# Output projection of a hybrid encoder block: element-wise work of the Strassen-like pairs on VectorE alone, the first pair's second tile loaded inside the attention

## The chip, the cores and the metric

The kernel runs on one core of one Trainium2 chip. The metric is the device time of one execution in microseconds (us). The core's engines are TensorE (PE; its weight loads appear as PEld), VectorE (DVE), ScalarE (ACT), GpSimd (POOL) and SyncE (SP), each with an instruction queue of its own, and 16 DMA engines that they issue to.

## The reference

One layer of an encoder on x of shape (1, 2048, 1024), all in float32:

```
xn = rmsnorm(x);  z = xn @ w_in                      # q, k, v, pool input, forget logits
fox  = forgetting_attention(q, k, v, f)              # 8 heads of 64 channels, causal
pool = multiscale_pool(p_in)                         # 512 channels
h = x + concat(fox, pool) @ w_out                    # the output projection, w_out (1024, 1024)
h = h + memory_cross_attention(rmsnorm(h), mem)      # 4 heads, 256 memory tokens
h = h + swiglu(rmsnorm(h))                           # 1024 -> 2816 -> 1024
```

The change lies in the fourth line, `h = x + concat(fox, pool) @ w_out`, and in the end of the attention ahead of it.

## The kernel before

**Precision.** Every float32 operand of a matmul is split into a rounded part (hi) and a remainder (lo): ACT casts the raw values into hi, then another engine forms lo = raw - hi (`split`, L199 and L55). A product is three matmuls for each of four blocks of 128 (`mm3`, L60 to L62: hi x hi, lo weights x hi, hi x lo).

**Output projection in pairs.** The 16 token tiles of 128 rows are taken in eight pairs of tiles (i, i + 4). With the tiles' fox halves (x11, x21) and pool halves (x12, x22) and the halves of w_out, a pair's 2x2 block product is formed with seven products in place of eight (a Strassen-Winograd scheme). It needs four sums of operands, formed anew for each pair in `pair_ops`:

- s1 = x21 + x22, s2 = s1 - x11, s3 = x11 - x21, s4 = x12 - s2;
- the weights' sums t1 to t4 were formed earlier in the kernel and stored to DRAM; `out_weights` loads t3, t4 and the block b22, and splits them; b11, b21, t1 and t2 are loaded and split in the attention's last units.

A pair's products, in PE's order, are: x11 by b11, x22 of the earlier pair by t4, x12 by b21, s4 of the earlier pair by b22, s2 by t2, s1 by t1, s3 by t3. Each is 12 matmuls of 128x512. Three PSUM banks a pair hold them: bank a takes x11, then s2, then s3, then (in the next pair) x22 on top of one another; bank b s1, then s4; bank c x12. So between these products a bank has to be read out. `begun` (L1326) adds a bank to the rows of x that were loaded into a tile o; `ended` (L1331) adds a further bank to it, and then POOL stores o (L1332) to `h1d` in DRAM. The output blocks are called o11, o12, o21 and o22 here (first or second tile, first or second half of the columns). o12 is begun after s2, o22 after s1, and both read banks that the next products go into.

**Where the operands lie.** `pair_raw` loads the four parts of a pair into one tile of 4 x 512 (`praw`, two buffers): x11, x12, x21, x22 in places 0 to 3 (`raw`). The sums are written over parts that are done with: s1 over x22, s3 over x21, s2 over place 0, s4 over place 1. s1 and s2 are formed on DVE, s3 and s4 on POOL (L1292, `tt(..., pool)`). hi and lo go into places ww0 to ww10 (`out_place`), in turn.

**The first pair.** Its first tile is loaded in the attention's last unit already (`load_first_pair`, into the upper half of a value tile v), and split nine steps later (`split_first_pair`); its operands x11 and x12 stay there. Its second tile is loaded by `pair_raw(0)` into `praw`, which gets the buffer of the last head's values and so has to wait for the attention's last matmul. The remainders of t4 and b22 are formed on POOL, those of t3 on DVE.

**What sets the order.** In the attention the order on DVE, ACT and SP is that of the program text; `later(n, fn)` puts a function n steps of that text's loop later. In the output projection only SP's order is that of the text (`in_order(EN.SP)`), PE's is so everywhere, and DVE, ACT and POOL are ordered by the scheduler that builds the program. Each engine then works through its queue strictly in order. On SP a load that waits for its buffer holds up all that follow. `x_rows` takes its tiles from six buffers, for o12 from two (`oh`), so its loads wait for stores of earlier pairs; the next pair's four loads stand behind them.

Of the kernel before, what the change touches and what calls it, by code (L numbers as in the profile page):

```python
# [8 lines left out]
F32 = mybir.dt.float32  # L9
F32R = mybir.dt.float32r  # L10
AF = mybir.ActivationFunctionType
ALU = mybir.AluOpType
# [4 lines left out]
P = 128  # L17
# [23 lines left out]
def block_kernel(ctx: ExitStack, tc: tile.TileContext, x, xT, memT, cols, rows, w_qkvf, w_p, w_pool, w_out,  # L41
# [4 lines left out]
    act, dve, pool, pe, sp = nc.scalar, nc.vector, nc.gpsimd, nc.tensor, nc.sync  # L46

    def opened(stack, name, bufs=1, **kw):
        return stack.enter_context(tc.tile_pool(name=name, bufs=bufs, reuse_waits="tile", **kw))

    def f(ap):
        return ap.bitcast(F32)

    def sub_hi(lo, src, hi, eng=None):
        (eng or dve).tensor_tensor(out=lo, in0=src, in1=f(hi), op=ALU.subtract)  # L55
# [51 lines left out]
    catT = [dr.tile([FOXW, 512], F32, name=f"catT{n}") for n in range(4)]  # L107
    poolT = [dr.tile([POOLW, 512], F32, name=f"poolT{n}") for n in range(4)]
# [84 lines left out]
    def split_gain(hi, lo, raw, gain):  # L193
        act.activation(hi, raw, AF.Copy, scale=gain)
        dve.scalar_tensor_tensor(out=lo, in0=raw, scalar=gain, in1=f(hi), op0=ALU.mult, op1=ALU.subtract)

    def split(hi, lo, raw, gain=None, eng=None):
        if gain is None:
            act.copy(hi, raw)  # L199
            sub_hi(lo, raw, hi, eng)  # L200
        else:
            split_gain(hi, lo, raw, gain)

    tt = lambda o, a_, b_, op, e_=dve: e_.tensor_tensor(out=o, in0=a_, in1=b_, op=op)
# [31 lines left out]
    with xstack, in_order(EN.DVE, EN.Activation, EN.Pool, EN.SP):  # L236
# [540 lines left out]
        hp = opened(hps, "hp")  # L777
# [12 lines left out]
    ob, first_pair = {}, {}  # L790
    pair_tiles = lambda p_: (8 * (p_ // 4) + p_ % 4, 8 * (p_ // 4) + p_ % 4 + 4)

    def load_part(raw, src, i):

        sp.dma_start(raw, src[i // 4][:, i % 4 * P:(i % 4 + 1) * P].rearrange("(k p) t -> p k t", p=P))

    def load_first_pair():
        v = hp.tile([P, NT, P], F32R, tag="v", name="v", bufs=2)
        raw = [f(v[:, 4 * n:4 * n + 4]) for n in range(2)]
        lo = hp.tile([P, 4, P], F32R, tag="cm", name="x12l", bufs=3)  # L800
        hi = hp.tile([P, 4, P], F32R, tag="cm", name="x12h", bufs=3)
        load_part(raw[0], catT, 0)
        load_part(raw[1], poolT, 0)
        first_pair["x11"] = v[:, 8:12], v[:, 12:16]
        first_pair["x12"] = hi[:], lo[:]
        return raw

    def split_first_pair(raw):
        first_pair["raw"] = [r.rearrange("p k t -> p (k t)") for r in raw]
        for r, nm in zip(raw, ("x11", "x12")):  # L810
            hi, lo = first_pair[nm]
            act.copy(hi, r)
            sub_hi(lo, r, hi)
            first_pair[nm] = tuple(t_.rearrange("p k t -> p (k t)") for t_ in (hi, lo))

    with ExitStack() as c0:
        tpool = opened(c0, "tpool")
# [8 lines left out]
        def later(n, fn):  # L826
            due.append([n, fn])
# [139 lines left out]
        def halves(pl):  # L967

            t_ = [slab(n, pl, F32R) for n in range(4)]
            return [(t_[n // 4][:, n % 4 * 512:(n % 4 + 1) * 512], t_[2 + n // 4][:, n % 4 * 512:(n % 4 + 1) * 512])  # L970
                        for n in range(8)]

        def load_out_quarters():

            parts = halves(hpa)
            for n, (hi, lo) in enumerate(parts):
                ob[("b11", "b21")[n // 4], n % 4] = hi, lo

                def load(n=n, hi=hi, lo=lo):
                    raw = spool.tile([P, 512], F32, tag="s0", name="wor", bufs=4)  # L980
                    sp.dma_start(raw[:], w_out[n * P:(n + 1) * P, :512])
                    later(14, lambda: split(hi, lo, raw[:], eng=pool))

                later(4 + 4 * n, load)

        def load_out_sums():
            parts = halves(hpb)
            for c in range(4):
                nm = ("t2", "t1")[c // 2]
                raw = spool.tile([P, 1024], F32, tag="s1", name="wos", bufs=4)  # L990
                sp.dma_start(raw[:].rearrange("p (k c) -> p k c", k=2), osum[nm][:, 2 * (c % 2):2 * (c % 2) + 2])
                for n in range(2 * c, 2 * c + 2):
                    ob[nm, n % 4] = hi, lo = parts[n]
                    later(11 + 3 * n, lambda hi=hi, lo=lo, v=raw[:, n % 2 * 512:(n % 2 + 1) * 512]: split(hi, lo, v))

        def all_scores():
            for un in units:
                h, b = un["u"]
                if b == (1 if h else 2) and h + 1 < H:
                    heads[h + 1] = load_head(h + 1, (hpa, hpb)[(h + 1) % 2])  # L1000
                if b == 3 and h + 1 < H:

                    heads[h + 1] += (load_values(h + 1),)
                elif h + 1 == H and b == 3:

                    load_out_quarters()
                un["head"] = heads[h]
                yield from score_items(un)
            raw = load_first_pair()
            later(9, lambda: split_first_pair(raw))  # L1010
            load_out_sums()

        def all_values():
# [232 lines left out]
    with ExitStack() as c0:  # L1246
# [16 lines left out]
        def out_weights(nm):  # L1263

            if nm == "t3":
                t_ = wdp.tile([P, 4, 512], F32, tag="wd", name="wor", bufs=1)
                raw = [t_[:, 2 * n:2 * n + 2] for n in range(2)]
            else:
                raw = [f(pair_place(n + (5 if nm == "t4" else 7))[:]) for n in range(2)]
            for n, r in enumerate(raw):  # L1270
                sp.dma_start(r, w_out[FOXW + n * B:FOXW + (n + 1) * B, 512:].rearrange("(k p) c -> p k c", p=P)
                             if nm == "b22" else osum[nm][:, 2 * n:2 * n + 2])
                for k in range(2):
                    t_ = obp.tile([P, 2, 512], F32R, name=f"o{nm}{2 * n + k}")
                    ob[nm, 2 * n + k] = t_[:, 0], t_[:, 1]
                    split(t_[:, 0], t_[:, 1], r[:, k], eng=dve if nm == "t3" else pool)

        def pair_raw(p_):
            v = hp.tile([P, 4, 512], F32, tag="v", name="praw", bufs=2)
            x11, x12, x21, x22 = raw = [v[:, n] for n in range(4)]  # L1280
            if p_ == 0:
                x11, x12 = first_pair.pop("raw")
            for n in range(0 if p_ else 2, 4):
                r = raw[n]
                load_part(r.rearrange("p (k t) -> p k t", k=4), (catT, poolT)[n % 2], pair_tiles(p_)[n // 2])
            return (x11, x12, x21, x22), raw

        def pair_ops(p_, parts, raw):

            x11, x12, x21, x22 = parts  # L1290
            x = {}
            tt = lambda o, a_, b_, op, e_=dve: e_.tensor_tensor(out=o, in0=a_, in1=b_, op=op)  # L1292

            def put(nm, src):
                x[nm] = out_place()
                split(*x[nm], src)

            if p_:
                put("x11", x11)
                put("x12", x12)  # L1300
            else:
                x.update(first_pair)
            put("x22", x22)
            tt(x22, x21, x22, ALU.add)
            tt(x21, x11, x21, ALU.subtract, pool)
            tt(raw[0], x22, x11, ALU.subtract)
            put("s2", raw[0])
            put("s1", x22)
            put("s3", x21)
            tt(raw[1], x12, raw[0], ALU.subtract, pool)  # L1310
            put("s4", raw[1])
            return x

        def product_o(ps, xop, wop, first):
# [89 lines left out]
    with mstack, ExitStack() as c0:  # L1404
# [67 lines left out]
        with in_order(EN.SP):  # L1472
# [5 lines left out]
            for n in range(2, NT + 1):  # L1478
# [349 lines left out]
```

## Time and profile before

| what | value |
|---|---|
| runs | 2582.59, 2586.41, 2586.48 us; median 2586.41 us |
| the profiled execution | 2578.56 us, its span 2576.9 us |
| busy of the span | PE 97%, PEld 84%, DVE 67%, ACT 50%, POOL 32% |
| mean granted clock of TensorE | 0.995 |
| the stretch in question | output projection, from 845.87 us (first product) to about 1036 us |

A line of the timeline gives the start and the duration in us, the engine, the line of the kernel, the operation, what is written and read (out<-in), the shape, how many are merged in the row, and in brackets the idle time before it and what ended that. A wait that is put down to DVE or ACT means that PE stood still until that instruction had finished. Names without numbers are tiles: `obk` the PSUM banks of the projection, `ww` the places of hi and lo, `praw` the raw parts, `ot` and `ob` the split t3 or t4 and b22, `o` the output rows. In PE's rows `qs` and `kh` are the weights b11, t2 and b21, t1 in the buffers of the attention's heads.

### The profile page before, as it was taken

To read this page: it belongs to the slowest core of one execution; us is meant where nothing else is said; L and a number is where in the kernel's file an instruction comes from. 1 tells how busy PE (TensorE), PEld (TensorE's weight loads), DVE (VectorE), ACT (ScalarE), POOL (GpSimd) and SP (SyncE) were. 2 spreads that over 40 slices of the span, in tenths; PEclk is the share of its full clock that TensorE was granted. 3 is DMA by queue.
4 is the path that set the end of the run, shared out by engine and by line. 5 is a ranking of instruction groups with operands and counts; after the bars stand their busy time and mean duration, and the time that the engine had idled before them with its cause. 6 is when DMAs were issued, how large, how long until landed. Compare 5 with 4: busy or idle time off the path is not lost.

```text
span 2576.9 us, 37301 instructions
## 1 busy us (share of the span) xinstructions
PE 2510.7 (97%) x12909; PEld 2154.4 (84%) x12909; DVE 1734.8 (67%) x2998; ACT 1299.4 (50%) x2487; POOL 822.0 (32%) x1135
## 2 busy tenths in 40 slices
PE   8999998999999899999999999999999999999998
PEld 8999997788887687888778888888888888888887
DVE  4466745899998754555877778756766666665554
ACT  5555446788889422655543433334543333333443
POOL 0022424455555522444424545430001222212000
PEclk9999999999999999999999999999999999999999
DMA  8755767645433546222465555447773323325665
GB/s 276 215 178 156 216 192 210 187 123 156 130 109 92 185 150 214 74 87 95 174 224 181 174 178 190 151 164 271 244 266 109 122 104 108 122 98 185 228 214 186
DMA packets 246766, 434.01 MB, mean 168 GB/s; under 512 B 30000, under 2 KB 119856, under 8 KB 238896
## 3 DMA queue, kind: packets, MB, share of 16 engines
q1 hardware_dynamic: 213104, 322.54, 39.5%
q0 software_dynamic: 33472, 109.08, 11.7%
q8 instruction: 102, 1.67, 0.3%
q14 instruction: 88, 0.72, 0.1%
HBM read 294.02 MB, written 137.50 MB: 167 GB/s over the span
## 4 chain that ended last, share of the span: by engine, by line
PE 49%; issue 8%; DVE 2%; ACT 1%; DMA 1%; POOL 1%; SPq 0%; POOLq 0%; DVEq 0%; ACTq 0%
PE bk L62 13%; PE bk L60 13%; PE bk L61 13%; PE mmps L60 2%; PE mmps L62 2%; PE mmps L61 2%; PE tp L1039 1%; DVE ww L55 0%; PE obk L60 0%; PE obk L61 0%; PE obk L62 0%; DMA xraw<-hTd 0%; POOL out_dram L1721 0%; DMA wqr<-in_w_mem_q_dram 0%; DMA h<-h1d 0%
## 5 line engine op out<-in xcount | busy, mean ns | idle before, releaser
L55 DVE TENSOR_TENSOR ww<-draw,ww 128x512 fp32r<-128x512 f32 x308 | 205.2, 702 | 155.6 <-ACT ww L199 155.1
L199 ACT CAST ww<-draw 128x512 fp32r<-128x512 f32 x308 | 179.5, 620 | 218.8 <-PE bk L62 174.5
L55 DVE TENSOR_TENSOR ww<-graw,ww 128x512 fp32r<-128x512 f32 x220 | 177.8, 815 | 105.9 <-ACT ww L199 105.5
L61 PE MATMUL bk<-ww,ww 128*128 128x512 f32 x616 | 239.6, 389 | 0.0
L60 PE MATMUL bk<-ww,ww 128*128 128x512 f32 x616 | 239.6, 389 | 0.0
L62 PE MATMUL bk<-ww,ww 128*128 128x512 f32 x616 | 239.6, 389 | 0.0
L199 ACT CAST ww<-graw 128x512 fp32r<-128x512 f32 x220 | 135.9, 622 | 181.8 <-PE bk L62 159.8
L55 DVE TENSOR_TENSOR pl<-tp,ph 128x512 fp32r<-128x512 f32 (+3 forms) x296 | 176.7, 599 | 27.8 <-ACT ph L952 26.0
L871 ACT ACTIVATE s<-s,mx 128x1024 f32<-128x1024 f32 (+2 forms) x192 | 173.6, 905 | 7.7 <-DVE mx L865 7.1
L936 PE MATMUL tp<-ident,s 128*128 128x128 f32 x1088 | 171.5, 273 | 3.4 <-DVE pl L55 3.0
L60 PE MATMUL zps<-wh,xhi 128*128 128x386 f32 x512 | 174.6, 341 | 0.0
L62 PE MATMUL zps<-wh,xl 128*128 128x386 f32 x512 | 173.7, 339 | 0.0
L61 PE MATMUL zps<-wl,xhi 128*128 128x386 f32 x512 | 173.2, 338 | 0.0
L952 ACT CAST ph<-tp 128x512 fp32r<-128x512 f32 (+3 forms) x296 | 148.7, 514 | 38.3 <-PE tp L936 32.8
L936 PEld LDWEIGHTS tp<-ident,s 128*128 128x128 f32 x1088 | 133.9, 141 | 31.6 <-DVE pl L55 6.6
L1721 POOL DMA_DIRECT2D out_dram<-o x32 | 17.3, 542 | 382.5 <-DVE o L1718 381.6
L62 PE MATMUL bk<-qs,ww 128*128 128x512 f32 x352 | 137.2, 390 | 1.1 <-DVE ww L55 1.1
L60 PE MATMUL bk<-qs,ww 128*128 128x512 f32 x352 | 137.9, 392 | 0.3 <-ACT s L1640 0.3
L61 PE MATMUL bk<-kh,ww 128*128 128x512 f32 x352 | 137.0, 389 | 0.0
L60 PE MATMUL bk<-kl,ww 128*128 128x512 f32 x352 | 136.9, 389 | 0.0
L61 PE MATMUL bk<-cb,ww 128*128 128x512 f32 x352 | 136.9, 389 | 0.0
L62 PE MATMUL bk<-kl,ww 128*128 128x512 f32 x352 | 136.9, 389 | 0.0
(613 smaller groups left out, 7261.9 us busy)
## 6 DMA issues: line engine op xcount, KB each, us to landing
graw<-in_w_gu_dram SPq DMA_DIRECT2D x44, 1024.0 KB, 5.4
draw<-in_w_down_dram SPq DMA_DIRECT2D x66, 256.0 KB, 4.3
xl<-in_xT_dram SPq DMA_DIRECT2D x64, 256.0 KB, 4.5
wdr<-in_w_down_dram SPq DMA_DIRECT2D x22, 512.0 KB, 4.6
jl<-in_x_dram SPq DMA_DIRECT2D x32, 256.0 KB, 7.0
vd<-cb SPq DMA_DIRECT2D x16, 512.0 KB, 3.5
cb<-cd SPq DMA_DIRECT2D x8, 1024.0 KB, 7.8
v<-vd SPq DMA_DIRECT2D x8, 1024.0 KB, 5.4
```

What stands on the lines that cost most here:

```text
L55: (eng or dve).tensor_tensor(out=lo, in0=src, in1=f(hi), op=ALU.subtract)
L60: pe.matmul(ps, lhsT=sh, rhs=mh, start=first, stop=False, skip_group_check=goes_on)
L61: pe.matmul(ps, lhsT=sh, rhs=ml, start=False, stop=False, skip_group_check=goes_on)
L62: pe.matmul(ps, lhsT=sl, rhs=mh, start=False, stop=last, skip_group_check=goes_on)
L199: act.copy(hi, raw)
L871: act.activation(s[:, sl], s[:, sl], AF.Exp, bias=ng, scale=-1.0, accum_out=l[:, q, g:g + 1])
L936: pe.transpose(tp[:, q * P:(q + 1) * P], unit["rows"][q][:, j * P:(j + 1) * P], ident[:])
L952: act.copy(ph[:, sl], tp[:, sl])
L1039: pe.transpose(tp[:, e_], src[:, q + e_], ident[:])
L1721: pool.dma_start(out[rows_, cs], o)
```

## The change

All element-wise work of the projection goes to DVE: the sums s3 and s4 of every pair (`tt` loses its engine argument) and the remainders of t4 and b22 (`split` without `eng`). The sums get places of their own: in the pairs from the second on s1 goes into a tile of the small pool `cm` (three buffers, used by the attention's masks before), s2 into place 0, s3 into place 2, s4 over x12. Their order in the text changes: the three sums s1, s3, s2 first, then the splits of s2, s1, s3 and x22.

For the first pair the parts of the second tile are loaded sixteen steps after the request of the first (`load_first_second`), inside the attention: x21 into a `cm` tile, x22 over the raw x12, which has been split by then. As s4 still needs the raw x12, `pair_raw(0)` loads that part again into `praw`, and the other three places take s1, s2 and s3.

```diff
     def split_first_pair(raw):
-        first_pair["raw"] = [r.rearrange("p k t -> p (k t)") for r in raw]
         for r, nm in zip(raw, ("x11", "x12")):
...
+    def load_first_second(raw):
+        x21 = hp.tile([P, 4, P], F32, tag="cm", name="x21", bufs=3)[:]
+        load_part(x21, catT, pair_tiles(0)[1])
+        load_part(raw[1], poolT, pair_tiles(0)[1])
+        first_pair["raw"] = [r.rearrange("p k t -> p (k t)") for r in (raw[0], x21, raw[1])]
...
             later(9, lambda: split_first_pair(raw))
+            later(16, lambda: load_first_second(raw))
...
-                    split(t_[:, 0], t_[:, 1], r[:, k], eng=dve if nm == "t3" else pool)
+                    split(t_[:, 0], t_[:, 1], r[:, k])
...
             if p_ == 0:
-                x11, x12 = first_pair.pop("raw")
-            for n in range(0 if p_ else 2, 4):
-                r = raw[n]
+                load_part(raw[1].rearrange("p (k t) -> p k t", k=4), poolT, pair_tiles(0)[0])
+                x11, x21, x22 = first_pair.pop("raw")
+                return (x11, raw[1], x21, x22), raw[2], (raw[0], raw[3])
+            for n, r in enumerate(raw):
                 load_part(r.rearrange("p (k t) -> p k t", k=4), (catT, poolT)[n % 2], pair_tiles(p_)[n // 2])
-            return (x11, x12, x21, x22), raw
+            return raw, hp.tile([P, 512], F32, tag="cm", name="s1r", bufs=3)[:], (raw[0], raw[2])
...
-            put("x22", x22)
-            tt(x22, x21, x22, ALU.add)
-            tt(x21, x11, x21, ALU.subtract, pool)
-            tt(raw[0], x22, x11, ALU.subtract)
-            put("s2", raw[0])
-            put("s1", x22)
-            put("s3", x21)
-            tt(raw[1], x12, raw[0], ALU.subtract, pool)
-            put("s4", raw[1])
+            tt(s1, x21, x22, ALU.add)
+            tt(s3, x11, x21, ALU.subtract)
+            tt(s2, s1, x11, ALU.subtract)
+            put("s2", s2)
+            put("s1", s1)
+            put("s3", s3)
+            put("x22", x22)
+            tt(x12, x12, s2, ALU.subtract)
+            put("s4", x12)
```

The order in which the engines' queues then stand is shown with the steps of the prediction. Lines after the new function have higher numbers: the sums move from L1292 to L1300, `begun` from L1326 to L1334, `ended` from L1331 to L1339.

More of the change, by code (lines that the diff above doesn't have):

```diff
@@ L1275, in out_weights, with pair_ops @@
                     ob[nm, 2 * n + k] = t_[:, 0], t_[:, 1]
-                    split(t_[:, 0], t_[:, 1], r[:, k], eng=dve if nm == "t3" else pool)
+                    split(t_[:, 0], t_[:, 1], r[:, k])
         def pair_raw(p_):
             v = hp.tile([P, 4, 512], F32, tag="v", name="praw", bufs=2)
-            x11, x12, x21, x22 = raw = [v[:, n] for n in range(4)]
+            raw = [v[:, n] for n in range(4)]
             if p_ == 0:
-                x11, x12 = first_pair.pop("raw")
-            for n in range(0 if p_ else 2, 4):
-                r = raw[n]
+                load_part(raw[1].rearrange("p (k t) -> p k t", k=4), poolT, pair_tiles(0)[0])
+                x11, x21, x22 = first_pair.pop("raw")
+                return (x11, raw[1], x21, x22), raw[2], (raw[0], raw[3])
+            for n, r in enumerate(raw):
                 load_part(r.rearrange("p (k t) -> p k t", k=4), (catT, poolT)[n % 2], pair_tiles(p_)[n // 2])
-            return (x11, x12, x21, x22), raw
-        def pair_ops(p_, parts, raw):
+            return raw, hp.tile([P, 512], F32, tag="cm", name="s1r", bufs=3)[:], (raw[0], raw[2])
+        def pair_ops(p_, parts, s1, free):
             x11, x12, x21, x22 = parts
+            s2, s3 = free
             x = {}
-            tt = lambda o, a_, b_, op, e_=dve: e_.tensor_tensor(out=o, in0=a_, in1=b_, op=op)
+            tt = lambda o, a_, b_, op: dve.tensor_tensor(out=o, in0=a_, in1=b_, op=op)
             def put(nm, src):
```

## The prediction, made before the changed kernel was run

> **What bounds the kernel now.** I read the page first, then the windows around the output projection, then PE's timeline there, and last DVE's.
>
> ```profile
> span 2576.9 us, 37301 instructions
> PE 2510.7 (97%) x12909; PEld 2154.4 (84%) x12909; DVE 1734.8 (67%) x2998; ACT 1299.4 (50%) x2487; POOL 822.0 (32%) x1135
> 850.00:860.00 10.00, 4.90 (x15) 3.35 (x14) 8.63 (x12) 5.14 (x9) 4.59 (x5) 0.83 0.83 273
> 860.00:870.00 10.00, 9.24 (x33) 6.91 (x32) 4.37 (x7) 5.70 (x10) 8.69 (x7) 0.83 1.04 310
> 960.00:970.00 10.00, 7.35 (x32) 5.73 (x31) 8.09 (x12) 2.39 (x4) 4.18 (x5) 0.96 0.21 79
> 970.00:980.00 10.00, 10.00 (x40) 8.14 (x39) 2.48 (x4) 1.31 (x3) 0.54 (x1) 0.87 0.79 233
> ```
>
> PE is busy for 97% of the span, so only time in which PE waits or runs slowly can be won. The windows' columns are length, then busy time of PE, PEld, DVE, ACT and POOL, the granted clock, the DMA share and GB/s. Around 850 PE loses half of a window, and the clock falls to 0.83; around 965 it happens again, less. Both places lie in the output projection. These are its starts of products, and what PE waited for:
>
> ```profile
> 845.87 0.39 PE L60 MATMUL obk<-qs,v 128*128 128x512 f32 x1
> 855.14 0.50 PE L60 MATMUL obk<-qs,ww 128*128 128x512 f32 x1 [3.65 <-ACT ww L199]
> 857.32 0.79 PE L62 MATMUL obk<-qs,ww 128*128 128x512 f32 x1 [1.44 <-DVE ww L55]
> 868.06 0.50 PE L60 MATMUL obk<-qs,ww 128*128 128x512 f32 x1
> 869.55 0.50 PE L62 MATMUL obk<-qs,ww 128*128 128x512 f32 x1 [0.76 <-DVE ww L55]
> 888.75 0.50 PE L60 MATMUL obk<-ot,ww 128*128 128x512 f32 x1 [3.04 <-DVE o L1326]
> 910.64 0.39 PE L60 MATMUL obk<-qs,ww 128*128 128x512 f32 x1
> 929.68 0.39 PE L60 MATMUL obk<-qs,ww 128*128 128x512 f32 x1
> 947.04 0.50 PE L60 MATMUL obk<-ot,ww 128*128 128x512 f32 x1 [0.88 <-DVE o L1326]
> 969.05 0.69 PE L60 MATMUL obk<-ot,ww 128*128 128x512 f32 x1 [2.65 <-DVE o L1326]
> 973.50 0.40 PE L60 MATMUL obk<-qs,ww 128*128 128x512 f32 x1
> 1011.91 0.50 PE L60 MATMUL obk<-ot,ww 128*128 128x512 f32 x1 [1.98 <-DVE o L1326]
> ```
>
> From 910.64 to 929.68 lies pair 3 with its seven products: 19.04 us without a wait, so 2.72 us a product. From the first product (845.87) to that of s3 in pair 7 (1011.91) stand 53 products, 144.2 us, and 0.8 us of transposes; it took 166.0, so 21.0 us are lost. By place: 8.6 up to 868.06, where pair 1 begins five products after the start, and about 1.1 in the product there (0.76 and two start-ups); 3.2 in pair 1 (3.04 and a start-up of 0.2); 1.1 and 2.9 in pairs 4 and 5; 1.7 after that, since the product at 969.05 took 4.45 us and not 2.72 (the 0.87 of the windows); 2.2 in pair 7.
>
> **Why PE waits.** From pair 1 on every wait is for the evacuation L1326 of the output block o12 (first tile, second half of the columns), ahead of the product of s3, which goes into the same bank. DVE works strictly in its order, and o12 stands behind the next pair's splits. Pair 5, with pair 6's splits:
>
> ```profile
> 955.70 0.69 DVE L55 TENSOR_TENSOR ww<-praw,ww 128x512 fp32r<-128x512 f32 x1 [4.89 <-ACT ww L199]
> 959.84 0.69 DVE L55 TENSOR_TENSOR ww<-praw,ww 128x512 fp32r<-128x512 f32 x1 [0.99 <-ACT ww L199]
> 960.56 0.69 DVE L1292 TENSOR_TENSOR praw<-praw 128x512 f32<-128x512 f32 x1
> 962.72 0.69 DVE L1292 TENSOR_TENSOR praw<-praw 128x512 f32<-128x512 f32 x1 [1.46 <-POOL praw L1292]
> 963.93 2.07 DVE L55 TENSOR_TENSOR ww<-praw,ww 128x512 fp32r<-128x512 f32 x2
> 967.12 0.68 DVE L1331 TENSOR_TENSOR o<-obk,o 128x512 f32<-128x512 f32 x1
> 967.72 0.68 DVE L55 TENSOR_TENSOR ww<-praw,ww 128x512 fp32r<-128x512 f32 x1
> 968.32 1.28 DVE L1326 TENSOR_TENSOR o<-obk,o 128x512 f32<-128x512 f32 x2
> 924.33 0.68 DVE L1331 TENSOR_TENSOR o<-obk,o 128x512 f32<-128x512 f32 x1
> 945.11 0.68 DVE L1331 TENSOR_TENSOR o<-obk,o 128x512 f32<-128x512 f32 x1
> L55 DVE TENSOR_TENSOR ww<-praw,ww x54: 675/688/1785, 850.5 to 1005.4; 128x512 fp32r<-128x512 f32 x54
> L1292 POOL TENSOR_TENSOR praw<-praw x14: 1282/1294/1624, 873.9 to 984.3; 128x512 f32<-128x512 f32 x14
> ```
>
> x22's split comes at 959.84, s1 at 960.56; then DVE waits 1.46 us for POOL's s3 before it may form s2, and the two splits at 963.93 take 2.07 us (1.29 without hindrance), one of them stretched while POOL forms s4. The last two rows (min, median and max in ns) say the same: a DVE split is 688 ns, up to 1785 beside a POOL sum of 1294. So o12 comes 8.5 us after x22's split. The other two L1331 rows are the last evacuation of the earlier pair's block (924.33, 945.11, 967.12): 20.8 and 22.0 us apart, while PE needs 19.04 a pair. Its store frees the buffer behind whose load the next operands queue on SP. DVE therefore falls back by some 1.8 us a pair until PE waits.
>
> **The change, part by part.**
>
> *Sums on DVE, kept apart.* In pairs 1 to 7 POOL loses two sums (1.29 us each), DVE gets two (0.69, started 0.60 apart: 967.12, 967.72, 968.32). DVE then has seven splits, four sums and seven evacuations, 18 x 0.60 = 10.9 of 19.04 us: not the bound. The order on DVE in pair 5 before (from x11's evacuation of pair 5, o_12383, to o12, o_12385; praw_12514 is pair 6's data):
>
> ```order
> L1326 TENSOR_TENSOR o_12383<-obk_12414,o_12383 128x512
> L55 TENSOR_TENSOR ww9_12531<-praw_12514,ww9_12531 128x512
> L1292 TENSOR_TENSOR praw_12514<-praw_12514 128x512 x2
> L1326 TENSOR_TENSOR o_12442<-obk_12278,o_12442 128x512
> L55 TENSOR_TENSOR ww6_12411<-praw_12378,ww6_12411 128x512
> L55 TENSOR_TENSOR ww0_12540<-praw_12514,ww0_12540 128x512
> L1331 TENSOR_TENSOR o_12383<-obk_12416,o_12383 128x512
> L55 TENSOR_TENSOR ww1_12543<-praw_12514,ww1_12543 128x512
> L1331 TENSOR_TENSOR o_12249<-obk_12279,o_12249 128x512
> L55 TENSOR_TENSOR ww10_12537<-praw_12514,ww10_12537 128x512
> L1326 TENSOR_TENSOR o_12385<-obk_12414,o_12385 128x512
> ```
>
> and after, the same stretch (o_12390 to o_12392; s1 into s1r_12526 stands in the row ahead of it):
>
> ```order
> L1334 TENSOR_TENSOR o_12390<-obk_12421,o_12390 128x512
> L1300 TENSOR_TENSOR praw_12521<-praw_12521 128x512
> L1300 TENSOR_TENSOR praw_12521<-s1r_12526,praw_12521 128x512
> L55 TENSOR_TENSOR ww0_12548<-praw_12521,ww0_12548 128x512
> L1334 TENSOR_TENSOR o_12449<-obk_12284,o_12449 128x512
> L55 TENSOR_TENSOR ww9_12542<-praw_12521,ww9_12542 128x512
> L1300 TENSOR_TENSOR praw_12521<-praw_12521 128x512
> L1339 TENSOR_TENSOR o_12390<-obk_12423,o_12390 128x512
> L55 TENSOR_TENSOR ww1_12551<-praw_12521,ww1_12551 128x512
> L1339 TENSOR_TENSOR o_12255<-obk_12285,o_12255 128x512
> L55 TENSOR_TENSOR ww10_12545<-s1r_12526,ww10_12545 128x512
> L1334 TENSOR_TENSOR o_12392<-obk_12421,o_12392 128x512
> ```
>
> The sums moved in, x22's split moved from ahead of s1 to behind s4, and nothing in the chain waits for POOL. From s1's start to o12 there are now 12 steps, 12 x 0.605 = 7.3 us, and to the earlier block's last evacuation 10 steps, 6.1 us. s1 can start when x22 has landed, about 0.7 before its split, at 959.1: o12 at 966.4 instead of 968.3, the evacuation at 965.2 instead of 967.1. That one takes back the 1.8 us a pair by which DVE falls behind, so the delay no longer builds up. I take the waits of pairs 4 and 5 and the slow product as gone: -5.7 us (1.1 + 2.9 + 1.7); if the 1.9 us are won once and the delay stays, pair 4's 1.1 go and 1.9 of pair 5's: -3.0.
>
> *Weights' splits.* Eight remainders of t4 and b22 move from POOL to DVE, 8 x 0.60 = 4.8 us, ahead of pair 1's first splits. They wait for loads:
>
> ```profile
> 833.66 0.32 SPq L886 DMA_DIRECT2D ld<-li  x1
> 835.96 0.45 SPq L892 DMA_DIRECT2D lbs<-ld  x1
> 846.07 0.37 SPq L795 DMA_DIRECT2D praw<-catT  x1
> 846.49 0.50 SPq L795 DMA_DIRECT2D praw<-poolT  x1
> 847.30 1.88 DVE L55 TENSOR_TENSOR cb<-wos,kh 128x512 fp32r<-128x512 f32 x3
> 847.46 3.13 POOL L904 TENSOR_TENSOR fo<-fo,lbs 64x512 f32<-64x512 f32 x1 [3.53 <-DVE fo L898]
> 849.88 0.62 ACT L199 CAST ww<-praw 128x512 fp32r<-128x512 f32 x1 [1.66 <-DMA praw<-poolT]
> 850.88 0.57 POOL L906 DMA_DIRECT2D catT<-fo  x1 [0.29 <-POOL fo L904]
> SPq L1271 <- DMA catT<-fo: 5.9, 1, 5.9
> 868.21 0.62 ACT L199 CAST ww<-praw 128x512 fp32r<-128x512 f32 x1 [0.20 <-DMA praw<-poolT]
> ```
>
> SP holds the second half of t4 for 5.9 us behind the attention's last store (850.88), with b22 and pair 1's operands queued after it; the queue is full (DMA share 1.04), and x12 of pair 1 lands only at 868.2. The eight splits lie beside these loads, so I cost them at nothing, and pair 1 cannot start before about 868 either way; with faster loads up to 4.8 us of them would show.
>
> *Pair 1.* In the new order 23 steps stand between x11's split (868.2 and 0.6 of ACT) and o12: 13.9 us, 882.7, done at 883.4; PE would come to s3 at 888.75 - 3.2 = 885.5. The wait goes, -3.2. Pair 2's operands must land meanwhile; if they are 1.5 us late, -1.7.
>
> *Pair 0.* The loads of x21 and x22 go on SP between the last store of the inverse row sums (833.66) and their load back (835.96), where SP waits for 2.0 us; two issues of 0.37 and 0.50 fit in. Behind them stands only that load, which POOL needs at 847.46. At 846.07 one load (x12 again) is left of two. s1 can run as soon as the value tile is free, at 846, ahead of the attention's last evacuation, which it holds up by 0.1 at most. But DVE's order is new:
>
> ```order
> L55 TENSOR_TENSOR cb_11134<-wos_11139,kh_11132 128x512
> L55 TENSOR_TENSOR cb_11134<-wos_11141,kh_11132 128x512 x2
> L1300 TENSOR_TENSOR praw_11692<-v_11126,x21_11339 128x512
> L1300 TENSOR_TENSOR praw_11692<-praw_11692,v_11126 128x512
> L1300 TENSOR_TENSOR praw_11692<-praw_11692 128x512
> L55 TENSOR_TENSOR ww0_11718<-praw_11692,ww0_11718 128x512
> L55 TENSOR_TENSOR ww1_11721<-praw_11692,ww1_11721 128x512
> L55 TENSOR_TENSOR ww2_11724<-praw_11692,ww2_11724 128x512
> L55 TENSOR_TENSOR ww3_11727<-v_11126,ww3_11727 128x512
> L55 TENSOR_TENSOR ww4_11731<-praw_11692,ww4_11731 128x512
> L1334 TENSOR_TENSOR o_11694<-obk_11766,o_11694 128x512
> ```
>
> where before this stood:
>
> ```order
> L55 TENSOR_TENSOR cb_11134<-wos_11141,kh_11132 128x512 x2
> L55 TENSOR_TENSOR ww0_11713<-praw_11689,ww0_11713 128x512
> L1326 TENSOR_TENSOR o_11692<-obk_11764,o_11692 128x512
> L1292 TENSOR_TENSOR praw_11689<-praw_11689 128x512
> L1331 TENSOR_TENSOR o_11692<-obk_11766,o_11692 128x512
> ```
>
> The evacuation of the first product moved behind three sums and five splits, and the product of s2 goes into the same bank. From 849.2 (last weight split): 3 x 0.6 and 0.1, then 5 x 0.6 and the evacuation of 0.7: 854.9. PE comes to s2 at 855 and not at 856.6 (857.32 less two matmuls), unless POOL's scaling (847.46) takes its 1.4 us in the middle: 856.3. Both are hidden again, since pair 1 starts with its loads at 868: 0, with ends of -1.0 (256 KB less at the 273 GB/s of the window) and +1.4 (the store at 850.88 that much later).
>
> *Pair 7.* Its wait hangs on the mem-query weights, whose loads start when pair 5's last block is stored. Those come about a microsecond earlier: -0.4, ends -2.2 and 0.
>
> Sum: 0 - 3.2 - 5.7 - 0.4 = -9.3 us; ends -12.1 and -3.3. The profiled execution took 2578.56 us (span 2576.9): 2569.3 for one like it. The runs' median is 2586.41, 7.9 above it, for no reason that this trace shows; I set the sum against the median: 2577.1. About 0.2%, 5.2 us, can be told from no change here.
>
> **The rivals.**
>
> *The clock.* After 2.65 us of waiting the product at 969.05 ran slowly, after 3.04 the one at 888.75 did not (first matmul 0.50, not 0.69). The Trainium skill ("TensorE: Matmul & The Clock Gate", Part 1) has a free-running window of 3.4 us, and half the clock after an idle one. By it a wait's place in the window decides beside its length; the two rows bear that out, though a wholly idle window was not needed here. In pair 0 PE now works through s2, s1 and s3 without a break (8.2 us) and then stands idle in one piece until 868, from 863.1 or 864.5, where before the long wait lay ahead of s2 and the slow matmuls after it (0.79 at 857.32) were hidden by the loads. If that makes pair 1's first products slow, 1.7 us are lost, at most twice: -7.6 or -5.9, some 2579.5.
>
> *A new wait in place of the old.* x11's evacuation, which lets s2 begin, now stands behind s1, and s1 needs the second tile's loads landed. If they still land as late as in pair 5 (959.1, 9.3 us after that pair's first product at 949.8, 947.04 and a product), PE waits for it or for o12 by a microsecond in pairs 4 to 6: half the gain of these goes, -9.3 + 3 to 5, some 2582. For it speaks the full queue, against it the shorter cycle.
>
> *Slower.* If the loads land later than 8.3 us into a pair, o12 (7.3 + 0.7 after) misses the 16.3 us (six products) at which s3 is due. At 11.4 us in each of pairs 2 to 6 that is 5 x 3.1 = 15.5 lost against 9.3 won: 2592.6. It would need an evacuation two microseconds later than now, and the chain got shorter.
>
> *It does nothing.* If pair 1's and pair 5's waits were the loads' and not the chain's, 2586.
>
> **How the numbers follow.** Forecast (-12 to -7.5) 0.48; the clock 0.2; a new wait 0.2; nothing 0.07; slower 0.05. Faster by more than 5.2 us are the first, three quarters of the clock and a third of the new wait: 0.70; slower 0.05; the rest, 0.25, is the same. The range reaches from 2571 (all waits gone, and 3 us of scatter as between the runs) to 2584.
>
> **What would show it.** After: no POOL sums in the projection; PE's waits on o12 in pairs 1, 4 and 5 under 0.5 us together, the clock 1.00 from 880 to 1000; the last evacuations 19.0 us apart; s2 of pair 0 waiting for L1334, not ACT; pair 1 still beginning near 868. Wrong would be waits of over 1 us a pair on L1334, or a second stretch at half clock after 868.

## The result, and the profile after

| what | before | after |
|---|---|---|
| median of six runs, us | 2583.09 | 2572.61 |
| lowest to highest, us | 2580.55 to 2586.48 | 2571.55 to 2575.98 |
| profiled execution, its span, us | 2576.9 | 2570.0 |

The ratio of the runs is 0.9957, with an interval of 0.9947 to 0.9967: the changed kernel is about 11 us faster. Forecast were 9.3 us less. The forecast time of 2577.1 us was counted from 2586.41, the median of three runs of the kernel before; that of all six is 2583.09. So of the 4.5 us that the forecast time is too high, 3.3 come from that median.

The head of the page of the changed kernel, and four windows of it (length, busy time of PE, PEld, DVE, ACT and POOL, granted clock, DMA share, GB/s):

```profile
span 2570.0 us, 37278 instructions
PE 2510.6 (98%) x12909; PEld 2156.2 (84%) x12909; DVE 1736.8 (68%) x3022; ACT 1298.8 (51%) x2487; POOL 789.2 (31%) x1111
850.00:860.00 10.00, 5.42 (x20) 4.18 (x19) 9.56 (x14) 4.15 (x8) 4.67 (x3) 0.86 0.76 260
860.00:870.00 10.00, 9.64 (x34) 7.38 (x33) 7.05 (x12) 6.53 (x12) 0.00 (x0) 0.80 1.03 310
960.00:970.00 10.00, 10.00 (x46) 8.29 (x45) 3.34 (x6) 1.25 (x2) 1.08 (x2) 1.00 0.75 227
970.00:980.00 10.00, 10.00 (x46) 8.29 (x45) 8.31 (x13) 2.40 (x4) 1.62 (x3) 1.00 0.35 122
```

PE's own time is the same (2510.6 against 2510.7). The hole around 965 with its slow clock is gone, that around 855 is not. PE's starts of products, as they were shown of before:

```profile
847.63 0.40 PE L60 MATMUL obk<-qs,v 128*128 128x512 f32 x1
857.86 0.77 PE L60 MATMUL obk<-qs,ww 128*128 128x512 f32 x1 [4.58 <-DVE o L1334]
869.03 0.39 PE L60 MATMUL obk<-qs,ww 128*128 128x512 f32 x1
871.77 0.50 PE L62 MATMUL obk<-qs,ww 128*128 128x512 f32 x1 [2.13 <-DVE ww L55]
890.54 0.39 PE L60 MATMUL obk<-qs,ww 128*128 128x512 f32 x1
985.74 0.39 PE L60 MATMUL obk<-qs,ww 128*128 128x512 f32 x1
1002.96 0.39 PE L60 MATMUL obk<-ot,ww 128*128 128x512 f32 x1
```

These two are the waits of over 0.3 us that are left; in pair 0 the slow clock is left too. From 890.54 to 985.74 pass five pairs in 95.2 us, 19.04 each. From the first product to s3 of pair 7 it is 155.3 us, before 166.0: 10.7 less. The span fell by only 6.9, since the attention ended 1.8 us later in this execution and the rest behind s3 of pair 7 took 2.1 longer. Neither can be put down to the change from these two profiles: in one of the experiments below, whose kernel is that of before up to the projection, the first product came at 848.25, in another of that kind at 845.89, and the rest varied from 1564.8 to 1569.1 us over all runs. With the early load the first product came at 846.8 to 850.8, without it at 845.9 to 848.3; whether that load delays the attention's end stays open. The experiments are compared by this stretch, beside the time. It is that of one execution each, while the runs of one kernel lie 4 to 14 us apart.

### The profile page after: what moved, and what is told of

It is laid out like the page before. It is cut to its first block, busy times and chain, and to the rows that moved or that the text cites. A ratio compares the mean times of both kernels' runs of the same rounds, so it can differ in the third digit from the quotient of the medians.

```text
span 2570.0 us, 37278 instructions
## 1 busy us (share of the span) xinstructions
PE 2510.6 (98%) x12909; PEld 2156.2 (84%) x12909; DVE 1736.8 (68%) x3022; ACT 1298.8 (51%) x2487; POOL 789.2 (31%) x1111
## 4 chain that ended last, share of the span: by engine, by line
PE 67%; issue 9%; DVE 2%; ACT 2%; POOL 1%; DMA 1%; SPq 0%; POOLq 0%; DVEq 0%; ACTq 0%
PE bk L62 13%; PE bk L60 13%; PE bk L61 13%; PE acc L926 5%; PE sps L863 5%; PE tp L941 4%; PE obk L62 2%; PE obk L60 2%; PE obk L61 2%; PE mmps L60 2%; PE mmps L62 2%; PE mmps L61 2%; PE tp L1045 1%; DVE ww L55 0%; DMA xraw<-hTd 0%
## 5 line engine op out<-in xcount | busy, mean ns | idle before, releaser
L61 PEld LDWEIGHTS bk<-ww,ww 128*128 128x128 f32 x616 | 115.7, 188 | 24.2 <-DVE ww L55 0.4
```

Source lines behind the costliest of these rows:

```text
L61: pe.matmul(ps, lhsT=sh, rhs=ml, start=False, stop=False, skip_group_check=goes_on)
```

## The experiments

Theory A was that DVE lost its time waiting for POOL's sums, B that the places were at fault, C that the early load helps.

**The sums alone on DVE.**

```diff
-            tt(x21, x11, x21, ALU.subtract, pool)
+            tt(x21, x11, x21, ALU.subtract)
...
-            tt(raw[1], x12, raw[0], ALU.subtract, pool)
+            tt(raw[1], x12, raw[0], ALU.subtract)
```

> The kernel before, with s3 and s4 formed on DVE instead of POOL, still over the parts x21 and x12; the loads, the places and the weights' remainders are as before. Theory A (the delay came from DVE waiting for POOL's two sums in each pair): PE's waits ahead of s3 in pairs 1, 4, 5 and 7 (8.6 us in all) and the 1.7 us at half clock go, and the time falls by 8 to 11 us, to about 2573. Theory B (it is the places: with s1 over x22, x22's split still stands ahead of s1, and the earlier block's last evacuation still behind it): at most half of it, 2578 or more. Theory C (it is the second tile loaded in the attention): no change, 2583.

**The new places and order, with s3 and s4 on POOL.** The early load and the weights' remainders on DVE stay in it.

```diff
-            tt(s3, x11, x21, ALU.subtract)
+            tt(s3, x11, x21, ALU.subtract, pool)
...
-            tt(x12, x12, s2, ALU.subtract)
+            tt(x12, x12, s2, ALU.subtract, pool)
```

> The changed kernel, with s3 and s4 formed on POOL again; the places, the early load and the weights' remainders on DVE stay. Theory A: DVE waits for POOL again, but s2 no longer waits for s3, which has a place of its own, so only the stretched splits (up to 1.8 in place of 0.69 us) and s4 are left: part of the gain is lost, 2575 to 2580, with waits of PE on o12 of 1 to 5 us in all in pairs 1, 4, 5 and 7. Theory B: nothing is lost, 2573. Theory C: nothing is lost, 2573.

**Without the early load.**

```diff
-            later(16, lambda: load_first_second(raw))
...
-                load_part(raw[1].rearrange("p (k t) -> p k t", k=4), poolT, pair_tiles(0)[0])
-                x11, x21, x22 = first_pair.pop("raw")
-                return (x11, raw[1], x21, x22), raw[2], (raw[0], raw[3])
+                for n in (2, 3):
+                    load_part(raw[n].rearrange("p (k t) -> p k t", k=4), (catT, poolT)[n % 2], pair_tiles(0)[1])
+                x11, x12 = first_pair.pop("raw")
+                return (x11, x12, raw[2], raw[3]), raw[0], (raw[1], raw[2], raw[3])
...
```

> The changed kernel without the early load: the first pair's second tile is loaded by pair_raw(0) as in the kernel before, s1, s2, s3 and s4 of that pair go into the four places of that tile. Theory A: the early load is worth nothing beside pair 1's loads, 2571 to 2575, pair 1 beginning within 1 us of where it does in the changed kernel, counted from the first product (21.4 us). Theory B: the same. Theory C: the gain goes, 2580 to 2583.

**The early load alone**, in the kernel before (the same lines put in, the sums as they were).

> The kernel before, with the first pair's second tile loaded in the attention's last unit and x12 loaded again, as in the changed kernel; s1 and s3 of that pair alone have places of their own; the sums s3 and s4 stay on POOL in all pairs and the weights' remainders too. Theory A: no gain, 2581 to 2585, with the waits of pairs 4, 5 and 7 as before. Theory B: the same. Theory C: 2573.

| kernel | median us | ratio to before | interval | stretch us |
|---|---|---|---|---|
| before (stretch from its profile above) | 2582.94 | | | 166.0 |
| sums alone | 2580.82 | 0.9991 | 0.9982 to 0.9999 | 165.3 |
| places, sums on POOL | 2581.41 | 0.9996 | 0.9988 to 1.0005 | 165.1 |
| without the early load | 2573.45 | 0.9961 | 0.9948 to 0.9974 | 157.3 |
| early load alone | 2584.76 | 1.0008 | 0.9999 to 1.0017 | 167.3 |

Theory C falls: the early load alone gains nothing, and without it the gain is there. But A and B fall too as I had put them. Each half of the change alone gives some 2 us at most, both together 10 (the second half with the early load, which gains nothing, and with the weights' remainders). That calls for something with a threshold, and it shows where SP issues a pair's first load (praw<-catT). Before, and with the sums alone:

```profile
929.04 0.39 SPq L795 DMA_DIRECT2D praw<-catT  x1
937.83 0.69 DVE L55 TENSOR_TENSOR ww<-praw,ww 128x512 fp32r<-128x512 f32 x1 [1.04 <-ACT ww L199]
938.56 0.69 DVE L1292 TENSOR_TENSOR praw<-praw 128x512 f32<-128x512 f32 x1
945.11 0.68 DVE L1331 TENSOR_TENSOR o<-obk,o 128x512 f32<-128x512 f32 x1
949.92 0.39 SPq L795 DMA_DIRECT2D praw<-catT  x1
```

```profile
931.54 0.39 SPq L795 DMA_DIRECT2D praw<-catT  x1
941.64 1.42 DVE L1292 TENSOR_TENSOR praw<-praw 128x512 f32<-128x512 f32 x2
947.43 0.68 DVE L1331 TENSOR_TENSOR o<-obk,o 128x512 f32<-128x512 f32 x1
952.45 0.39 SPq L795 DMA_DIRECT2D praw<-catT  x1
```

With the new places and order, sums on POOL:

```profile
931.94 0.38 SPq L795 DMA_DIRECT2D praw<-catT  x1
940.82 0.69 DVE L1300 TENSOR_TENSOR s1r<-praw 128x512 f32<-128x512 f32 x1 [0.94 <-DMA praw<-poolT]
942.98 0.69 DVE L1300 TENSOR_TENSOR praw<-s1r,praw 128x512 f32<-128x512 f32 x1 [0.86 <-POOL praw L1300]
947.16 0.68 DVE L1339 TENSOR_TENSOR o<-obk,o 128x512 f32<-128x512 f32 x1
951.86 0.38 SPq L795 DMA_DIRECT2D praw<-catT  x1
```

And in the changed kernel:

```profile
925.75 0.38 SPq L795 DMA_DIRECT2D praw<-catT  x1
933.60 0.69 DVE L1300 TENSOR_TENSOR s1r<-praw 128x512 f32<-128x512 f32 x1 [0.35 <-DMA praw<-poolT]
939.91 0.69 DVE L1339 TENSOR_TENSOR o<-obk,o 128x512 f32<-128x512 f32 x1
944.63 0.38 SPq L795 DMA_DIRECT2D praw<-catT  x1
```

This is a ring: the loads, s1, the last evacuation of o12, its store, the load of o12's rows into that buffer two pairs on, and behind it on SP the next loads. The turn shown takes 20.9 us before, 20.9 with the sums alone, 19.9 with the sums on POOL and 18.9 in the changed kernel, where PE needs 19.04 a pair. The means of four turns, from the loads of pair 3 to those of pair 7, are 20.9, 20.9, 20.0 and 19.2. What is over 19.04 a turn runs up until PE waits.

The turn shown falls into parts, in us. The lead is the time by which the loads are issued ahead of the first product of the pair that runs then; landed means that the last of the four loads has landed.

| kernel | lead | until landed | from there to s1 | s1 to last evacuation | from there to next loads |
|---|---|---|---|---|---|
| before | 0.6 | 7.8 | 1.7 | 6.5 | 4.8 |
| sums alone | 0.1 | 8.6 | 1.5 | 5.8 | 5.0 |
| sums on POOL | 0.1 | 8.8 | 0.1 | 6.3 | 4.7 |
| changed kernel | 2.9 | 7.8 | 0.1 | 6.3 | 4.7 |

Where s1 overwrites x22, it starts 1.5 to 1.7 us behind the landing, because x22's cast and split come first (937.83, waiting for ACT); with a place of its own it starts 0.1 behind. The sums on DVE shorten only the next part, and in the old order alone. With the new places and order the ring from the landing on is the same with the sums on POOL and on DVE, although s2 waits 0.86 us for POOL: what differs is the landing, 8.8 against 7.8 us, and the lead. With the sums on POOL the lead was gone from the loads of pair 3 on (issued at 892.51, pair 2's first product at 892.57); in the changed kernel those were issued at 887.29, ahead of 890.54. In the turn before, o12's last evacuation stood 5.7 us behind s1 with the sums on POOL, with a wait of 0.86 us for POOL and a stretched row of three splits (2.99 us) between them, and 1.9 us in the changed kernel. That the sums on POOL cost the lead there is read from this one trace, not tested. So the new places bring the turn down to PE's pace, or nearly, and only as long as the loads keep a lead. By these traces that is why neither half gains much alone.

The ring can be cut without touching an engine, and that tells it from a chain on DVE that is too long by itself. Four other kernels come first.

**The weights' remainders on POOL**, in the changed kernel.

```diff
-                    split(t_[:, 0], t_[:, 1], r[:, k])
+                    split(t_[:, 0], t_[:, 1], r[:, k], eng=dve if nm == "t3" else pool)
```

> The changed kernel with the remainders of t4 and b22 formed on POOL again. The prediction costed them at nothing on DVE: then 2572 to 2574, and pair 1 begins where it does in the changed kernel (21.4 us after the first product). Rival: in the changed kernel x11's split of pair 1 (871.04) stands behind b22's splits and PE waits 2.13 us for it; on POOL this wait falls to 0.5 to 1.0 and 1 to 1.5 us are won. Other rival: four more POOL operations of 1.3 us beside DVE stretch DVE's splits, and 1 to 2 us are lost.

Measured: 2576.46 us, ratio 0.9969 (0.9957 to 0.9981), stretch 160.9. x11's wait in pair 1 did fall, from 2.13 to under 0.6. The stretching that the third expectation names is there too, in pair 1: s1 took 1.63 us and a split 1.77, beside POOL's splits that ended at 875.95, in place of 0.68 each. But pair 1 still took 0.7 us less than in the changed kernel; the loss lies in pairs 3 to 7, and no expectation had that: PE waited again for evacuations in pairs 1, 4, 5 and 7. The ring of this kernel:

```profile
929.65 0.38 SPq L795 DMA_DIRECT2D praw<-catT  x1
938.47 0.69 DVE L1300 TENSOR_TENSOR s1r<-praw 128x512 f32<-128x512 f32 x1 [0.96 <-DMA praw<-poolT]
945.07 0.68 DVE L1339 TENSOR_TENSOR o<-obk,o 128x512 f32<-128x512 f32 x1
949.93 0.38 SPq L795 DMA_DIRECT2D praw<-catT  x1
```

Its waits of PE from 845 to 1015 (us in total, times, longest; the longest is pair 0's, the others are the four):

```profile
PE obk L60 <- DVE o L1334: 9.8, 5, 4.6
```

From pair 4 on DVE's order is that of the changed kernel, and yet a turn takes 20.3 us: 8.8 from the issue to s1 and not 7.9, and 6.6 from there. s1 follows the landing by 0.1 us here too; it is the landing that is later, 8.7 us. What differs is when the loads start. In the changed kernel they are issued 2.8 to 3.3 us ahead of a pair's first product and s1 comes 7.8 to 8.4 later; here they began 1.9 ahead (889.54, pair 2's first product at 891.44), slid to the pair's beginning within two pairs, and s1 came 8.7 to 9.5 later. So the ring holds its lead or loses it, here by 1.4 us at pair 3's loads. Which transfers the loads meet at the later time wasn't tested.

**x22's split ahead of s1 in the text**, s1 in its own place.

```diff
+            put("x22", x22)
             tt(s1, x21, x22, ALU.add)
...
-            put("x22", x22)
             tt(x12, x12, s2, ALU.subtract)
```

> The changed kernel with x22's split written ahead of s1 in the text again, as before; s1 keeps its own place, the sums stay on DVE. Theory P (it is the place: since s1 no longer overwrites x22, it may run as soon as x22 has landed): as the changed kernel, 2571 to 2575, a load of operands every 19.0 us and no wait on o12 in pairs 2 to 6. Theory T (it is the order of the text): x22's split holds up s1, loads every 20 us or more as with the sums alone moved (20.8), 2578 to 2581.

Measured: 2574.69 us, 0.9958 (0.9946 to 0.9971), stretch 158.0. By the time it is the place (P). s1 follows the landing by 0.1 us in every turn, so for s1 the place is enough. In the trace the loads kept their lead of 3 us for pairs 3 and 4, then it fell to 0.1 for pair 7, with turns of 19.6 to 21.0. With x22's split first, 6.7 us lie between s1 and the last evacuation in three of its turns, 0.4 more than in the changed kernel: by this trace the order counts too.

**The first pair's order by hand.** The lines are those of the sums, splits and evacuations of pair 0, in this order on DVE and ACT:

```diff
+            tt(s1, x21, x22, ALU.add)
+            tt(s2, s1, x11, ALU.subtract)
+            put("s2", s2)
+            product_o(a, cur["x11"], "b11", True)
+            o11 = begun(a, i, 0, o_[0])
+            put("s1", s1)
...
```

> The changed kernel with the first pair's element-wise work in an order written out by hand: s1, s2, s2's split, x11's evacuation, s1's split, s3, its split, x22's split, and so on. Theory L (pair 1's loads bind, as the prediction had it): PE's wait of 4.58 us ahead of s2 goes to under 1, but pair 1 begins no earlier than 20 us after the first product (21.4 now) and the time falls by 0 to 1.5 us. Theory D (the evacuation that moved behind the splits binds): pair 1 begins 4 to 6 us earlier, about 2567.

**And the loads earlier.** In addition the last unit's scaling goes to DVE, pair 1's loads ahead of b22's on SP, and b22's splits behind those of x11 and x12:

```diff
-            pool.tensor_tensor(out=fo[:]...
+            (dve if unit is units[-1] else pool).tensor_tensor(out=fo[:]...
...
+            next_raw = pair_raw(1)
+            b22 = out_weights("b22")
...
```

> As the run with the first pair's order by hand, and three things more: the last unit's scaling on DVE right after its sum, so that the loads held up by it go earlier; pair 1's operands loaded ahead of b22; b22's splits behind those of x11 and x12 of pair 1. Theory L: with the loads earlier pair 1 begins 15 to 17 us after the first product, and the stretch to s3 of pair 7 falls from 155.3 to 149 to 151: about 2567. If the loads bind by their bytes (DMA share 1.0 from 858 on) and not by their start: 19 to 20 us, about 2571.

The first gave 2573.14 us (ratio 0.9958, 0.9945 to 0.9970) and a stretch of 155.9, the second 2570.38 us (0.9953, 0.9940 to 0.9966) and 155.6; neither is told apart from the changed kernel. Pair 1 began 22.2 and 20.7 us after the first product, in the changed kernel 21.4. The rows are PE's waits there, by the two kernels:

```profile
870.49 0.79 PE L60 MATMUL obk<-qs,ww 128*128 128x512 f32 x1 [5.88 <-ACT ww L199]
```

```profile
853.91 0.47 PE L60 MATMUL obk<-qs,ww 128*128 128x512 f32 x1 [1.45 <-DVE o L1337]
867.57 0.80 PE L60 MATMUL obk<-qs,ww 128*128 128x512 f32 x1 [2.80 <-ACT ww L199]
857.01 0.37 SPq L795 DMA_DIRECT2D praw<-catT  x1
864.41 1.14 ACT L199 CAST ot<-ww 128x512 fp32r<-128x512 f32 x2 [1.42 <-DMA ww<-wo_t]
```

So theory L holds: with s2's wait of 4.58 us taken away, PE waits that much ahead of pair 1 instead. And starting the loads earlier moves little: t4, issued by 854.1, is cast only at 864.41, in windows with a DMA share of 0.91 to 1.07 from 858 to 866. Until pair 1 the transfers' bytes bind, the second of the outcomes that I had named.

**The ring cut.** Three buffers for o12's rows in place of two, five for the others in place of six; in the kernel before, in the one with the weights' remainders on POOL, in the changed kernel, and in the last version:

```diff
-        def x_rows(i, a, tag="o", bufs=6):
+        def x_rows(i, a, tag="o", bufs=5):
...
-                o_ = x_rows(i, 0), x_rows(i, 1, "oh", 2), x_rows(i2, 1)
+                o_ = x_rows(i, 0), x_rows(i, 1, "oh", 3), x_rows(i2, 1)
```

> The kernel before with three buffers for the rows of o12 in place of two, and five for the other rows in place of six (the same memory); nothing else is changed, POOL forms s3 and s4. Theory R (a ring binds: loads of operands, s1, last evacuation of o12, its store, the load of o12's rows into that buffer, the next loads behind it; 20.8 us a turn against PE's 19.04): the ring is cut, PE's waits in pairs 4, 5 and 7 and the half-rate product go (8 us), the wait in pair 1 may stay: about 2575. Rival Q (DVE's chain with POOL's sums is too long by itself): waits as before, 2583.

> The changed kernel with the remainders of t4 and b22 on POOL, and the buffers of the run before this one. With two buffers it lost 3 us of the gain: its ring began one microsecond later in pair 3, the loads then took 9 us and not 8.2 to s1, and it fell back to PE's pace in two pairs. Theory R: with the ring cut that loss goes, 2571 to 2574, no wait on o12 from pair 2 on. Rival Q (POOL's eight splits themselves cost it): 2576 to 2577.

> The changed kernel with the same buffers. Theory R: no wait is left from pair 2 on in the changed kernel, so nothing is won, 2571 to 2574; pair 0 and pair 1 keep their 10 us. Rival Q: the same.

> The version with the first pair's order by hand, the last scaling on DVE and pair 1's operands loaded ahead of b22, with the same buffers. Its loss lies up to pair 1's s3, where the loads bind by their bytes: 2569 to 2572, the stretch from the first product to s3 of pair 7 within 1 us of 155.6, unless the earlier loads of pair 2 that the buffers allow collide with those of pair 1 and b22, then up to 2 us more.

| with the ring cut | median us | ratio to before | interval | stretch us |
|---|---|---|---|---|
| kernel before | 2576.19 | 0.9975 | 0.9964 to 0.9985 | 159.4 |
| weights' remainders on POOL | 2571.80 | 0.9953 | 0.9941 to 0.9966 | 157.0 |
| changed kernel | 2575.24 | 0.9965 | 0.9953 to 0.9978 | 156.2 |
| first pair by hand, loads earlier | 2568.85 | 0.9945 | 0.9931 to 0.9959 | 157.3 |

The kernel before with the ring cut, first its timeline, then one of its groups from 845 to 1036 (busy time, mean ns, idle time ahead):

```profile
888.54 0.79 PE L60 MATMUL obk<-ot,ww 128*128 128x512 f32 x1 [3.00 <-DVE o L1326]
902.95 0.39 SPq L795 DMA_DIRECT2D praw<-catT  x1
922.00 0.81 SPq L795 DMA_DIRECT2D praw<-catT  x1
941.02 0.39 SPq L795 DMA_DIRECT2D praw<-catT  x1
```

```profile
L1292 DVE TENSOR_TENSOR praw<-praw 128x512 f32<-128x512 f32 x15 | 10.4, 691 | 9.3 <-POOL praw L1292 9.1
```

POOL still forms s3 and s4, and DVE waits 9.3 us for it, as in the kernel before (10.4, 692 and 9.3 there). But the loads go out every 19.0 us, 9 us ahead of a pair, and after pair 1's wait of 3.00 PE waits for no evacuation any more. s1 comes 1.6 us into a pair there (913.50, pair 3's first product at 911.91), in the kernel before 8.9 (938.56, pair 4's at 929.68). So two numbers that touch no engine win 0.25%, where the change wins 0.43%. One reservation: the scheduler, which sees the earlier loads, also placed some evacuations earlier in DVE's queue, so buffers and order were not parted.

The second line of the table agrees with the ring (2571.8 after 2576.5; the intervals overlap). The changed kernel gained nothing with it, as expected; its median is even higher, with a new wait of 0.4 us on an evacuation (L1339) in pair 4. The same wait is 0.7 us in the second kernel of the table and 1.4 in the last; why it comes wasn't tested. The last version has the lowest median of all, but its interval overlaps that of the changed kernel, and its stretch is that of its slowest execution (2575.43). The 1.7 us by which that stretch is longer than 155.6 are not the collision of loads that I had named: up to pair 2 it took 43.1 us, with and without the third buffer, and pair 4 with its wait took 20.7 us in place of 19.0.

## Why the prediction was right, point by point

*Pair 0, costed 0 (-1.0 to +1.4).* Right in its places. s2 waited for L1334 and began 10.2 us after the first product (forecast 855 or 856.3, that is 9.1 or 10.4), and POOL's scaling did come in between:

```profile
849.21 4.33 POOL L909 TENSOR_TENSOR fo<-fo,lbs 64x512 f32<-64x512 f32 x1 [4.45 <-DVE fo L903]
852.17 1.93 DVE L1300 TENSOR_TENSOR praw<-praw 128x512 f32<-128x512 f32 x1
857.03 0.68 DVE L1334 TENSOR_TENSOR o<-obk,o 128x512 f32<-128x512 f32 x1
869.23 0.69 DVE L1339 TENSOR_TENSOR o<-obk,o 128x512 f32<-128x512 f32 x1 [0.83 <-PE obk L62]
869.84 1.28 DVE L55 TENSOR_TENSOR ob<-ww,ob 128x512 fp32r<-128x512 f32 x2
871.04 1.28 DVE L55 TENSOR_TENSOR ww<-praw,ww 128x512 fp32r<-128x512 f32 x2
```

The sum s4 took 1.93 us beside the scaling, and the scaling 4.33 in place of 3.13. Pair 1 began at 869.03, 0.8 earlier after the first product than before.

*The weights' splits, costed 0.* The term missed what stands behind them. x11's split of pair 1 (871.04) came after o22's evacuation, which waits for PE, and two of b22's splits; PE waited 2.13 us, before 0.76. With pair 0 this makes +0.5, so two misses nearly cancel here. That on POOL they make the stretch 5.6 us longer (the medians differ by 3.9), with the loss in pairs 3 to 7 and so through the ring, the prediction didn't see.

*Pair 1, -3.2.* Right: s3 began without a wait, 18.8 us after the pair's first product, before 20.7 (of pair 1's gain 1.3 went to x11's wait).

*Pairs 4 and 5, -5.7.* Right in size: no wait, clock 1.00. Right in part in its reason. The group of splits from 845 to 1036, before and after:

```profile
L55 DVE TENSOR_TENSOR ww<-praw,ww 128x512 fp32r<-128x512 f32 x54 | 45.2, 856 | 23.2 <-ACT ww L199 23.2
```

```profile
L55 DVE TENSOR_TENSOR ww<-praw,ww 128x512 fp32r<-128x512 f32 x46 | 31.2, 686 | 13.0 <-ACT ww L199 12.5
```

The stretched splits are gone (856 to 686 ns). I had 1.9 us for a turn, 1.5 from s1's earlier start and the rest from the chain. s1 came 9.5 us after the loads' issue before (938.56) and 7.9 after, 1.6 less; the loads had landed after 7.8 us in both, so the 1.6 are what s1 no longer waits for x22's split, about the 1.5 that I had. From s1 to the earlier block's last evacuation it took 6.5 and 6.3, where I had 0.4 less. What I did not have is that the landing goes with the lead: with the weights' remainders on POOL the same order, with a lead of 1.9 us that was soon gone, gave turns of 19.9 to 20.5 us. DVE's wait for POOL was not what bound by itself, as the cut ring shows with its reservation; the turn of 20.9 us was. Of it I had the drift (1.8 us a pair) and the way back through store and SP, but not that PE's pace is a threshold for it, with gains that don't add.

*Pair 7, -0.4.* This is the term that was mis-sized. From pair 7's first product to s3 it took 17.2 us, before 19.4: -2.2, the far end of my range. The place was right, the size not:

```profile
987.25 0.68 DVE L1331 TENSOR_TENSOR o<-obk,o 128x512 f32<-128x512 f32 x1
991.91 1.48 SPq L1372 DMA_DIRECT2D wqr<-in_w_mem_q_dram  x3
```

```profile
977.78 0.69 DVE L1339 TENSOR_TENSOR o<-obk,o 128x512 f32<-128x512 f32 x1 [0.17 <-PE obk L62]
982.49 1.33 SPq L1380 DMA_DIRECT2D wqr<-in_w_mem_q_dram  x3
```

The first load of mem-query weights went 0.6 us ahead of pair 7's first product (992.55) before, and 3.3 ahead (985.74) after. I had said one microsecond earlier, where the drift that ends gives 2.6. The other kernels lie on the same line: 0.1 ahead (sums on POOL) 20.2 us, 1.7 (sums alone) 17.9, 3.1 (without the early load) 17.2.

With what was measured the sum is +0.5 - 3.2 - 5.7 - 2.2 = -10.6, the stretch gave -10.7. *The rivals:* the clock did fall in pair 0 (0.77 at 857.86, a clock of 0.80), hidden by the loads as I had it; the first matmul of pair 1 was not slow here, but in both versions by hand it was (0.79 and 0.80). First matmuls after a wait of 3.00 and 2.80 us were slow, after 3.04 before not: by these rows the length of a wait alone doesn't decide it. The Trainium skill ("TensorE: Matmul & The Clock Gate", Part 1) has a free-running window of about 3.4 us and half the clock after an idle one. That a wait's place counts beside its length fits the rows; that a whole window must be idle doesn't, since both slow waits were shorter than 3.4 us. *The new wait* didn't come in the changed kernel. With the weights' remainders on POOL something like it did: s1 came 8.7 us into pair 4 (938.47 after 929.73), and PE waited 0.8 and 1.1 us for o12 in pairs 4 and 5.

## What to carry to other kernels

Where PE waits a little longer pair after pair, look for a ring through buffers and queues, write down its turn, and compare it with PE's own time: what shortens a turn gains little until it falls to that, and a turn can depend on the lead with which it starts. Two halves that each gain little can then be worth all of it together, and one buffer more at the right place, paid for by one less elsewhere, can be worth as much as moved work.

## What was not expected of the hardware

The same four loads of 256 KB, from the same queue, landed 7.8 to 8.3 us after their issue in the changed kernel, where that was some 3 us ahead of a pair, and 8.6 to 9.4 where it was less than 0.8 ahead (weights' remainders on POOL). The kernel before has an exception, 7.8 us with a lead of 0.6. With the later landing the ring did not get its lead back; which transfers the loads meet then stays open. The scaling of 64 x 512 elements took POOL 4.33 us beside DVE's sums, 3.13 in the kernel before, and DVE 1.06 in the version with the loads earlier, so POOL's time is no guide to what the work costs on DVE.
